# A contrast kernel's first tiles stored in pieces, later tiles loaded two to a DMA, one more sum shared

## The chip, the cores and the metric

The kernel runs on one core of a Trainium2 chip. The metric is the device time of one execution in microseconds (us); three runs of the kernel before gave 238.86, 238.88 and 239.06 us, median 238.88. Profiles are of one execution each and have their own time beside them. Engines are called by the profile's short names: PE is TensorE, DVE is VectorE, ACT is ScalarE, POOL is GpSimd, SP is SyncE. A DMA is issued by an engine's queue (here SP's and ACT's) and carried out by sixteen DMA engines that the queues share.

## What is computed

```python
# x: 16 x 3 x 512 x 512, float32; factor = 1.5
mean = np.mean(x, axis=(2, 3), keepdims=True)
return np.clip(mean + factor * (x - mean), 0, 1).astype(np.float32)
```

For each of 48 images of 262,144 pixels: the mean, then factor * x + (1 - factor) * mean, cut to the range 0 to 1. The input and the output have 50.33 MB each; every byte is read once and written once.

## The kernel before

The input is seen as 12 tiles of 128 partitions by 8192 numbers (`ROW`), 4 MB each. An image fills 32 partitions, so a tile holds four images. SBUF holds a ring of six tiles (`BUFS`); tile t lives in slot t % 6, is changed in place, and is stored from there. A load of tile t + 6 therefore has to wait until tile t has been stored.

A tile goes through these steps:

- `load` (L67 to L75): a DMA issued by SP, for one tile or, with n=2, for two tiles in neighbouring slots. In one for two tiles a partition's row of the first tile is followed by its row of the second, so that both land together.
- `add` (L87 to L91): one ACT pass, a copy onto itself, whose accumulator gives each partition's sum. For tile 0 the work is shared: DVE sums the first 4352 numbers of each partition (`SUM`, the reduction at L109), ACT the other 3840.
- `shift_by` (L93 to L97): PE multiplies the sums by a 128 x 128 matrix `blockw`, which has (1 - factor) / 262144 in four blocks of 32 x 32, so that each partition of the result `bias` in PSUM holds its image's (1 - factor) * mean. A shared sum takes two matmuls into one accumulator.
- `clip` (L77 to L85): two DVE passes, first factor * x + bias (L79), then the cut to 0 and 1 (L83).
- `store` (L99 to L100): a DMA issued by ACT's queue. ACT works its instructions in order, so a store that waits for DVE holds up the ACT pass behind it, and an ACT pass that waits for a load holds up the store behind it.

The order is written by hand (`tc.manual_schedule()`). At the start SP issues the loads of tile 0, of tile 1, of tiles 2 and 3 in one DMA, and of tiles 4 and 5 in one DMA. Tile 0 is then clipped and stored in three pieces of 4, 12 and 16 KB per partition (`CUTS`: columns 0 to 1024, to 4096, to 8192), with the ACT pass for the sum of tile 1 ahead of the last store; then SP issues the load of tile 6. The loop at L120 takes tiles 1 to 11: matmul, clip, the sum of the next tile on ACT, the store of this tile behind it, and the load of tile t + 6 alone. Waits between engines, for landings and for slots are put in by the framework, which also reuses eight semaphores for DMA completions.

Of the kernel before, what the change touches and what calls it, by code (L numbers as in the profile page):

```python
# [1 line left out]

# [4 lines left out]


P = 128  # L10
ROW = 8192
BUFS = 6
SHORT = 2048
CUTS = (0, SHORT // 2, 2 * SHORT, ROW)
SUM = 4352


@with_exitstack
def kernel(
    ctx: ExitStack,  # L20
    tc: tile.TileContext,
    x: bass.AP,
    factor: float,
    out: bass.AP,
):

    nc = tc.nc
    f32 = mybir.dt.float32  # L30
    Alu = mybir.AluOpType
    Act = mybir.ActivationFunctionType

    B, C, H, W = x.shape
    n_img, n_pix = B * C, H * W
    ppi = n_pix // ROW
    per_tile = P // ppi
    n_tiles = n_img // per_tile
    assert ppi * ROW == n_pix and per_tile * n_tiles == n_img

    factor = float(factor)
    wconst = (1.0 - factor) / float(n_pix)

    x_f = x.rearrange("b c h w -> (b c h w)")
    out_f = out.rearrange("b c h w -> (b c h w)")

    def dram(ap, t, c0=0, c1=ROW):
        return bass.AP(tensor=ap.tensor, offset=t * P * ROW + c0, ap=[[ROW, P], [1, c1 - c0]])

    consts = ctx.enter_context(tc.tile_pool(name="consts", bufs=1))  # L50
    xpool = ctx.enter_context(tc.tile_pool(name="xpool", bufs=1))
    small = ctx.enter_context(tc.tile_pool(name="small", bufs=1))
    psum = ctx.enter_context(tc.tile_pool(name="psum", bufs=1, space=bass.MemoryType.PSUM))


    sums = small.tile([P, 2 * n_tiles], f32, name="sums")
    bias = psum.tile([P, n_tiles], f32, name="bias")

    blockw = consts.tile([P, P], f32, name="blockw")
    nc.gpsimd.memset(blockw, 0.0)  # L60
    for a in range(0, P, ppi):
        nc.gpsimd.memset(blockw[a : a + ppi, a : a + ppi], wconst)  # L62


    ring = xpool.tile([P, BUFS, ROW], f32, name="ring")

    def load(t, c0=0, c1=ROW, n=1):  # L67

        b = t % BUFS
        src = bass.AP(  # L70
            tensor=x_f.tensor,
            offset=t * P * ROW + c0,
            ap=[[ROW, P], [P * ROW, n], [1, c1 - c0]],
        )
        nc.sync.dma_start(out=ring[:, b : b + n, c0:c1], in_=src)  # L75

    def clip(t, c0, c1):  # L77
        part = ring[:, t % BUFS, c0:c1]
        nc.vector.tensor_scalar(  # L79
            out=part, in0=part, scalar1=factor, scalar2=bias[:, t : t + 1],  # L80
            op0=Alu.mult, op1=Alu.add,
        )
        nc.vector.tensor_scalar(  # L83
            out=part, in0=part, scalar1=0.0, scalar2=1.0, op0=Alu.max, op1=Alu.min
        )  # L85

    def add(t, c0=0):  # L87
        part = ring[:, t % BUFS, c0:ROW]
        own = sums[:, 2 * t : 2 * t + 1]
        nc.scalar.activation(out=part, in_=part, func=Act.Copy, accum_out=own)  # L90
        return own  # L91

    def shift_by(t, *parts):  # L93
        for k, part in enumerate(parts):
            nc.tensor.matmul(  # L95
                bias[:, t : t + 1], blockw, part, start=k == 0, stop=k == len(parts) - 1
            )  # L97

    def store(t, c0, c1):  # L99
        nc.scalar.dma_start(out=dram(out_f, t, c0, c1), in_=ring[:, t % BUFS, c0:c1])  # L100

    with tc.manual_schedule():
        load(0)
        load(1)
        load(2, n=2)
        load(4, n=2)

        rest = sums[:, 1:2]
        nc.vector.tensor_reduce(  # L109
            out=rest, in_=ring[:, 0, 0:SUM], axis=mybir.AxisListType.X, op=Alu.add  # L110
        )
        shift_by(0, add(0, SUM), rest)
        for c0, c1 in zip(CUTS[:-2], CUTS[1:-1]):
            clip(0, c0, c1)
            store(0, c0, c1)
        clip(0, CUTS[-2], ROW)
        own = add(1)
        store(0, CUTS[-2], ROW)
        load(BUFS)
        for t in range(1, n_tiles):  # L120
            shift_by(t, own)
            clip(t, 0, ROW)
            if t + 1 < n_tiles:
                own = add(t + 1)
            store(t, 0, ROW)
            if t + BUFS < n_tiles:
                load(t + BUFS)


# [1 line left out]
_INS = ['x', 'factor']  # L131
_OUTS = [((16, 3, 512, 512), 'float32')]

_NUMBERS = {'factor': 1.5}


# [26 lines left out]
```

## Time and profile before

| what | value |
|---|---|
| median of three runs | 238.88 us |
| the profiled execution's time / its span | 238.96 / 237.2 us |
| moved by DMA | 100.66 MB, mean 424 GB/s |
| busy: DVE / ACT / PE | 112.1 / 82.9 / 7.6 us |
| last load issued / landed | 162.46 / 195.23 us |
| last store issued / landed | 212.10 / 236.35 us |

The span runs from the first to the last instruction; the rest of an execution's time lies around it. In the page, part 3 gives each DMA queue's packets, megabytes, and the time that its packets took as a share of sixteen engines' span. An answer by windows gives for each stretch its length, the busy time of PE, PEld, DVE, ACT and POOL with the number of instructions, the granted clock, the mean share of the DMA engines that was busy, and GB/s. A line of the timeline gives start, duration, engine, source line, operation, output and input, and in brackets the idle time before it with what ended it. Line numbers of the form L79 are those of the kernel before.

### The profile page before, as it was taken

The numbers are of one execution on the slowest core, as the hardware profiler recorded it, in microseconds if no ns is written. First come the engines' busy times: TensorE is split into PE (matmuls) and PEld (weight loads), VectorE is DVE, ScalarE is ACT, GpSimd is POOL, SyncE is SP. The second block draws the span as 40 slices with busy tenths as digits, with TensorE's granted clock in tenths as the row PEclk, the third lists the DMA queues.
The fourth block names the chain that finished last, engine by engine and source line by source line (L and its number), as shares of the span: only waits on it lengthen the run. The fifth ranks groups of instructions, "written<-read, shape, count | busy, mean of one in ns | idle before, by whom it ended". The sixth has DMA issues, their size and how long they took to land.

```text
span 237.2 us, 219 instructions
## 1 busy us (share of the span) xinstructions
PE 7.6 (3%) x26; PEld 6.5 (3%) x26; DVE 112.1 (47%) x29; ACT 82.9 (35%) x25; POOL 0.9 (0%) x9
## 2 busy tenths in 40 slices
PE   0010000000000000000000000000000000000000
PEld 0010000000000000000000000000000000000000
DVE  0079668008991039979408605902920940770000
ACT  2050910199200696470190083065038009100000
POOL 1000000000000000000000000000000000000000
DMA  7999998999999999999999999999999999999996
GB/s 265 442 442 443 398 473 381 419 456 409 470 387 420 431 442 442 442 442 442 442 437 392 420 431 442 442 442 442 442 437 431 403 420 431 442 442 442 442 442 265
DMA packets 3713, 100.66 MB, mean 424 GB/s; under 512 B 385, under 2 KB 385, under 8 KB 513
## 3 DMA queue, kind: packets, MB, share of 16 engines
q1 hardware_dynamic: 1696, 50.33, 49.7%
q10 hardware_dynamic: 2016, 50.33, 49.2%
q14 instruction: 1, 0.00, 0.0%
HBM read 50.33 MB, written 50.33 MB: 424 GB/s over the span
## 4 chain that ended last, share of the span: by engine, by line
DMA 53%; another core or an unknown queue 14%; DVE 11%; issue 9%; PE 1%; ACT 1%; SPq 0%; ACTq 0%
DMA ring<-in_x_dram 33%; DMA out_dram<-ring 20%; DVE ring L79 6%; DVE ring L83 6%; PE bias L95 1%; ACT ring L90 1%; SPq L75 0%; ACTq L100 0%; ACTq L90 0%
## 5 line engine op out<-in xcount | busy, mean ns | idle before, releaser
L90 ACT ACTIVATE ring<-ring 128x8192 f32<-128x8192 f32 (+1 forms) x12 | 80.7, 6725 | 118.8 <-DMA ring<-in_x_dram 111.5
L79 DVE TENSOR_SCALAR ring<-ring,bias 128x8192 f32<-128x8192 f32 (+3 forms) x14 | 54.3, 3881 | 86.5 <-PE bias L95 86.5
L83 DVE TENSOR_SCALAR ring<-ring 128x8192 f32<-128x8192 f32 (+3 forms) x14 | 53.4, 3818 | 0.5
L95 PE MATMUL bias<-sums,blockw 128*128 128x1 f32 x26 | 7.6, 361 | 195.5 <-ACT ring L90 194.9
L95 PEld LDWEIGHTS bias<-sums,blockw 128*128 128x128 f32 x26 | 6.5, 311 | 196.5 <-ACT ring L90 179.3
L109 DVE TENSOR_REDUCE sums<-ring 128x1 f32<-128x4352 f32 x1 | 4.7, 4686 | 12.9 <-DMA ring<-in_x_dram 12.9
L90 ACT ACTIVATION_READ_ACCUMULATOR ring<-ring 128x1 f32 x12 | 2.2, 186 | 0.0
L90 ACT ACT_TABLE_LOAD x1 | 1.3, 1283 | 0.7 <-PEq L144 0.7
L62 POOL MEMSET blockw<- 32x32 f32 x4 | 0.5, 116 | 0.2
L60 POOL MEMSET blockw<- 128x128 f32 x1 | 0.2, 204 | 0.3 <-POOLq L144 0.3
L144 POOL MEMSET const-bfloat16-1.0<- 128x1 bf16 x1 | 0.1, 111 | 0.0
L144 POOL MEMSET const-uint8-127<- 128x1 uint8 x1 | 0.1, 111 | 0.0
L144 POOL MEMSET const-float32-1.0<- 128x1 f32 x1 | 0.1, 108 | 0.0
L144 POOL MEMSET const-float32-0.0<- 128x1 f32 x1 | 0.1, 103 | 0.2 <-issue 0.2
## 6 DMA issues: line engine op xcount, KB each, us to landing
out_dram<-ring ACTq DMA_DIRECT2D x11, 4096.0 KB, 44.7
ring<-in_x_dram SPq DMA_DIRECT2D x8, 4096.0 KB, 32.7
ring<-in_x_dram SPq DMA_DIRECT2D x2, 8192.0 KB, 60.8
out_dram<-ring ACTq DMA_DIRECT2D x1, 2048.0 KB, 37.3
out_dram<-ring ACTq DMA_DIRECT2D x1, 1536.0 KB, 26.2
out_dram<-ring ACTq DMA_DIRECT2D x1, 512.0 KB, 16.1
```

The lines of the kernel that those rows point to most:

```text
L60: nc.gpsimd.memset(blockw, 0.0)
L62: nc.gpsimd.memset(blockw[a : a + ppi, a : a + ppi], wconst)
L79: nc.vector.tensor_scalar(out=part, in0=part, scalar1=factor, scalar2=bias[:, t : t + 1], op0=Alu.mult, op1=Alu.add,)
L83: nc.vector.tensor_scalar(out=part, in0=part, scalar1=0.0, scalar2=1.0, op0=Alu.max, op1=Alu.min)
L90: nc.scalar.activation(out=part, in_=part, func=Act.Copy, accum_out=own)
L95: nc.tensor.matmul(bias[:, t : t + 1], blockw, part, start=k == 0, stop=k == len(parts) - 1)
L109: nc.vector.tensor_reduce(out=rest, in_=ring[:, 0, 0:SUM], axis=mybir.AxisListType.X, op=Alu.add)
L144: nc = _bacc.Bacc("TRN2", target_bir_lowering=False, num_devices=1)
```

## The change

- Tile 0 is stored in four pieces of 4, 8, 12 and 8 KB per partition, tile 1 in two of 16 KB, tile 2 in two of 20 and 12 KB. `CUTS` is now a table by tile.
- All loads after the first two are DMAs of two tiles: the loads of tiles 6 and 7, 8 and 9, 10 and 11 are issued together, after the store of tile 1, 3 and 5.
- The sum of tile 10 (the eleventh) is shared between DVE and ACT, as that of tile 0 is.
- The order on ACT's queue differs. The stores of tiles 0 to 2 and of the odd tiles come ahead of the next tile's sum, except the last piece of tile 0, which stays behind the sum of tile 1. The stores of even tiles from 4 on come behind the next tile's sum. The sum of tile 1 now stands behind the third piece of tile 0 and not the second.

```diff
-SHORT = 2048
-CUTS = (0, SHORT // 2, 2 * SHORT, ROW)
+CUTS = {0: (0, 1024, 3072, 6144, ROW), 1: (0, 4096, ROW), 2: (0, 5120, ROW)}
...
-    def shift_by(t, *parts):
+    def share(t):
+        rest = sums[:, 2 * t + 1 : 2 * t + 2]
+        nc.vector.tensor_reduce(
+            out=rest, in_=ring[:, t % BUFS, 0:SUM], axis=mybir.AxisListType.X, op=Alu.add
+        )
+        return [add(t, SUM), rest]
+
+    def shift_by(t, parts):
...
+    def pieces(t):
+        cuts = CUTS.get(t, (0, ROW))
+        return zip(cuts, cuts[1:])
...
-        rest = sums[:, 1:2]
-        nc.vector.tensor_reduce(
-            out=rest, in_=ring[:, 0, 0:SUM], axis=mybir.AxisListType.X, op=Alu.add
-        )
-        shift_by(0, add(0, SUM), rest)
-        for c0, c1 in zip(CUTS[:-2], CUTS[1:-1]):
-            clip(0, c0, c1)
-            store(0, c0, c1)
-        clip(0, CUTS[-2], ROW)
-        own = add(1)
-        store(0, CUTS[-2], ROW)
-        load(BUFS)
-        for t in range(1, n_tiles):
+        own = share(0)
+        for t in range(n_tiles):
             shift_by(t, own)
-            clip(t, 0, ROW)
-            if t + 1 < n_tiles:
-                own = add(t + 1)
-            store(t, 0, ROW)
-            if t + BUFS < n_tiles:
-                load(t + BUFS)
+            for c0, c1 in pieces(t):
+                clip(t, c0, c1)
+                if t % 2 or t in CUTS:
+                    if t == 0 and c1 == ROW:
+                        own = [add(1)]
+                    store(t, c0, c1)
+            if 0 < t < n_tiles - 1:
+                own = share(t + 1) if t + 1 == n_tiles - 2 else [add(t + 1)]
+            if t % 2 == 0 and t not in CUTS:
+                store(t, 0, ROW)
+            if t % 2 and t + BUFS < n_tiles:
+                load(t + BUFS - 1, n=2)
```

## The prediction

> **What bounds the kernel now.** I read the page's queue table first, then the busy rows of two stretches, then the timeline around the first and last stores, then the DMA packet records of the trace (start, length and bytes of each). The page's third part, queue, packets, MB, share of the 16 DMA engines:
>
> ```profile
> q1 hardware_dynamic: 1696, 50.33, 49.7%
> q10 hardware_dynamic: 2016, 50.33, 49.2%
> ```
>
> q1 carries SP's loads, q10 ACT's stores. Together they hold the sixteen engines 98.9% of the span. Two long stretches (length, busy time by engine, granted clock, DMA share, GB/s):
>
> ```profile
> 4.00:196.00 192.00, 7.01 (x24) 6.01 (x24) 103.21 (x27) 75.18 (x23) 0.00 (x0) 1.00 1.00 432
> 196.00:234.00 38.00, 0.59 (x2) 0.50 (x2) 8.92 (x2) 6.44 (x2) 0.00 (x0) 1.00 0.99 429
> ```
>
> The rate is the same with loads and stores mixed and, after 196 us, with stores alone. In the packet records an engine moves one 32 KB row of one partition in 1.213 us, load or store, and the next starts 0.004 us before that ends: 1.209 us a row. With both queues filled, the two take turns row by row, and a DMA's closing 4-byte packet uses up a turn. From 1.75 us (first packet) to 236.00 us (last) no engine has a gap over 0.05 us. Of the rows, 96 loads and 96 stores to an engine, 192 x 1.209 = 232.1 us; the rest of 234.25 us is the staggered, slow first packets and two patches, at 34 to 38 and 64 to 67 us, where load rows ran long by 0.3 us per engine each.
>
> The tail, by the timeline:
>
> ```profile
> 195.31 7.03 ACT L90 ACTIVATE ring<-ring 128x8192 f32<-128x8192 f32 x1 [12.25 <-DMA ring<-in_x_dram]
> 195.36 0.34 ACTq L100 DMA_DIRECT2D out_dram<-ring  x1
> ...
> 207.64 4.43 DVE L83 TENSOR_SCALAR ring<-ring 128x8192 f32<-128x8192 f32 x1
> 212.10 0.34 ACTq L100 DMA_DIRECT2D out_dram<-ring  x1
> ```
>
> The last load lands at 195.23 us, the last store is issued at 212.10 and lands at 236.35; the store ahead of it lands only at 226.68. So the last store waits in its queue, not for its data. The chain of waits ends in those last instructions because it follows semaphores; the queues bind. Nothing here can gain unless it takes bytes or idle time from the DMA engines, and the only slack is the two patches, 0.6 us.
>
> **The change, part by part.** All sums go against the profiled execution, 238.96 us, with a span of 237.2 us; it stands 0.08 us above the median of 238.88.
>
> *Pieces of the first three tiles.* Rows of 4, 12, 16 and 32 KB take 0.159, 0.460, 0.611 and 1.213 us: in proportion to bytes plus 8.4 ns, 4 ns of it overlapped, so 4.4 ns a packet. Stores of tiles 0 to 2 go from 24 + 8 + 8 = 40 packets an engine to 32 + 16 + 16 = 64. That is 24 x 4.4 ns = 0.11 us, on the path. Closing packets stay the same in number (17 stores for 14, 7 loads for 10). VectorE gets six more passes over pieces (two each for one more piece of tiles 0, 1 and 2); a pass has about 0.2 us fixed (0.759 us for 1024, 4.491 for 8192), so 1.2 us in all, beside an engine that is idle more than half the span: nothing, as long as stores stay queued.
>
> *Order on ACT's queue.* Now the third piece of tile 0 goes out ahead of the sum of tile 1, which then starts at about 26.4 instead of 23.71 us; queued behind it are the fourth piece and, through the matmul, tile 1's clip. Tile 1's two stores are issued ahead of the sum of tile 2 (now its store sits behind that sum until 46.47, though its clip ended at 40.46). Estimate from the rows: issues of tile 0 at 19.8, 22.3, 26.0, 33.7, tile 1 at 39 and 43.7, tile 2 at 59.3 and 63.0. Tile 0's 32 turns alone last until about 72 us, so the store queue is never empty; cost 0. Were that cover gone, each microsecond without stores would only go to loads as long as those last (about 71 us).
>
> *Loads in pairs.* Turns are shared by rows, and small store rows give loads a larger share: tiles 4 and 5 land at about 71 instead of 78.87 us. The built order shows one new wait: the load of tiles 4 and 5 waits for tile 1's landing (a reused semaphore), so it is issued at 22.6 instead of 2.10. Behind it on SP stand only loads that wait longer; the 16 rows of tiles 2 and 3 fill q1 until 45: nothing. Then the load of 6 and 7 waits for both tile 0 and tile 1 to be stored (about 81 us); q1 is empty from 71 to 85, and q10 alone runs, with tiles 1 and 2 queued and tile 3 from 80 on. A single queue moves 429 GB/s, so an empty q1 costs nothing. The same for 8 and 9 (issued when tile 3 has landed, 120 us; tiles 4 and 5 issued at 97 and 106) and 10 and 11 (after tile 5, 155 us, with 8 and 9 still in the queue).
>
> *The tail, the one place where it is near.* After the last load lands, tiles 10 and 11 both have to be summed and clipped, while only what is queued covers them. Tile 9's store must end after the same work as before (96 load rows, 80 store rows): 217.01 less 0.36 from last packet to landing, plus 0.11, is 216.75. The last load: tile 3's store ends 80 rows earlier, 216.75 - 80 x 1.209 = 120.0, lands at 120.4, and the load of 8 and 9 is issued. How long until its rows run? The nearest row is the first store: issued at 19.79 into a busy engine, its first packets ran at 23.2 (two engines) and 24.2 to 24.6 (fourteen), so 3.4 to 4.8 us. From 123.8 to 125.2, 32 load rows alternate with some 30 store rows: 62 x 1.209 = 75.0, and 0.4 to the landing: 199.2 to 200.6. Then, as for tile 0, reduction, matmul and waits (12.89 to 18.27: 5.4), two passes (4.49 + 4.43 and gaps: 8.95), issue: 14.4 us, tile 10's store is issued at 213.6 to 215.0. Into an empty queue the first load needed 1.0 us on the first engine and 2.0 on the last (0.74 to 1.75 and 2.71). So its rows are ready between 214.6 and 217.0, against 216.75: room of 2.1 down to minus 0.3 us. I take the middle, 1 us of room, since fourteen of sixteen engines showed the long wait and most of them the short start. The shared sum is what makes the room: by ScalarE alone 7.03 + 0.19 and 0.86 for the matmul, some 2.6 us later. Tile 11: 8.95 us after tile 10, 223 to 224, while tile 10's store runs to 226.4: covered.
>
> Sum: 238.96 + 0.11 = 239.07, **239.1 us**, 0.1% above the median.
>
> **One rule against the row.** The three more stores could each cost a fixed time. In the trace, the first store's last packet is followed at once by a load row, the second store's packets by turns; no gap stands at any change of DMA. Uncovered, a change of DMA would cost 1.0 us from issue to first packet and 0.36 to the landing: 3 x 1.36 = 4.1 us, 243.1; the three loads saved give nothing back, since theirs is covered now. The Trainium skill, "DMA: Bandwidth & Descriptors", section "Anatomy of one DMA — SWDGE (gpsimd) path", gives about 2.0 us fixed to each DMA, and its "Rules for kernel authors" want 1 MiB or more in each, where the first pieces have 0.5 and 1; by that figure the estimate would be 6 us, 245. The trace so far disagrees, as the other queue covers it.
>
> **The rivals.**
>
> *A. The engines stay filled: 239.1.* For it: q10 has a backlog at every point of the sum, and each landing of before follows from turns of 1.209 us.
>
> *B. The tail runs dry: slower.* If the last load lands under 15.4 to 16.4 us (14.4 and 1.0 to 2.0) ahead of the end of tile 9's store, the engines idle between tiles 9 and 10. It decides at a landing later than 200.4 to 201.4. One more row of delay, 1.21 us on the middle, takes the room and about 0.2 more; two, 1.4 us. So 239.3 to 240.5, typically 239.8. Against: the slowest wait seen is already in the bounds.
>
> *C. The long load rows multiply: slower.* Both patches fell in loads of two tiles (2 of 2; none over 0.02 us in the single loads after the start), and both just when a store with small rows had ended and all sixteen engines read at once (2 of 3 such ends). If it is the pairs, five instead of two cost 3 x 0.3 = 0.9 us: 240.0. If it is the ends of small stores, one or two more: 239.4 to 239.7.
>
> *D. The patches vanish: 239.07 - 0.6 = 238.5*, the floor; that is 0.17% under the median, and more is not there to be had.
>
> *E. Each piece pays its own start: 243.1*, above.
>
> **The numbers.** A measurement of this kernel tells 0.2% (0.48 us: 238.40 and 239.36) from no change. Chances: A 0.50, B 0.22, C 0.20, D 0.05, E 0.03. B, C and E come out slower almost throughout (0.44 of 0.45, taken as 0.45); half of D, where the patches give a little more than they cost before, is faster by more than the bound, 0.03, and the rest joins A as no change, 0.52. Range 238.5 to 240.6: D below, the dear end of B and C above; outside are E, two causes at once, and more than two late rows.
>
> **What would show it.** Right: packets without a gap from 1.75 us to the end; tiles 4 and 5 land near 71, 6 and 7 near 115, 8 and 9 near 163, 10 and 11 near 200 us; tile 10's store is issued near 214 and tile 9's lands near 217; the rate is 432 GB/s in every stretch. B: a stretch near 216 us with a DMA share well under 1, and the last two stores later by as much. C: stretches under 410 GB/s more than twice, each inside a load of two tiles, or at the ends of pieces. E: gaps at each change of DMA before 80 us. I am wrong in the ground if rows of a pair or of small pieces take longer than their bytes say, or if a queue alone runs slower than 429 GB/s.

## The result: 0.63% slower, inside the range and beside the likeliest case

The changed kernel takes 240.42 us (median of six runs, 240.2 to 241.17) against 238.87 us in six runs of the kernel before: ratio 1.0063, 95% interval 1.0051 to 1.0074. The forecast was 239.1 us, no change; that is 1.3 us too low. The range of 238.5 to 240.6 holds the result. The profiled execution took 240.38 us with a span of 238.4, so the span grew by 1.2 of the 1.4 us. In this document a run's ratio is always to runs of the kernel before on the same chip, over undisturbed executions; only the kernel before with all loads of one tile had others, three of six at 252.1 to 253.2 us, its profiled one among them.

The changed kernel's page, part 3, the two queues:

```profile
q1 hardware_dynamic: 1648, 50.33, 49.6%
q10 hardware_dynamic: 2448, 50.33, 49.1%
```

and the same two stretches by windows:

```profile
4.00:196.00 192.00, 6.42 (x22) 5.51 (x22) 95.07 (x31) 67.27 (x20) 0.00 (x0) 1.00 1.00 430
196.00:234.00 38.00, 1.76 (x6) 1.51 (x6) 22.43 (x5) 10.51 (x4) 0.00 (x0) 1.00 1.01 436
```

Both queues together are still busy 98.7% of the span, and the DMA share is 1.00 in both stretches. So neither stretch was lost to idle engines. The tail by the timeline:

```profile
200.47 4.69 DVE L94 TENSOR_REDUCE sums<-ring 128x1 f32<-128x4352 f32 x1 [11.84 <-DMA ring<-in_x_dram]
...
214.94 9.15 ACTq L106 DMA_DIRECT2D out_dram<-ring  x2
219.28 4.43 DVE L82 TENSOR_SCALAR ring<-ring 128x8192 f32<-128x8192 f32 x1
```

The last load has landed at 200.45 us, tile 10's store is issued at 214.94 and tile 11's 9 us later (223.74); tile 9's store lands at 218.24. That is the forecast's timetable (200, 214, 217) to within 1.3 us, and nothing runs dry. But tile 9's store lands 1.2 us later than before (217.01), so most of the time was lost ahead of the tail.

The difference shows at the very end. Two windows of the kernel before, from 234 us on:

```profile
234.00:235.00 1.00, 0.00 (x0) 0.00 (x0) 0.00 (x0) 0.00 (x0) 0.00 (x0) 1.00 1.21 524
235.00:238.00 3.00, 0.00 (x0) 0.00 (x0) 0.00 (x0) 0.00 (x0) 0.00 (x0) 1.00 0.00 0
```

and of the changed kernel:

```profile
234.00:235.00 1.00, 0.00 (x0) 0.00 (x0) 0.00 (x0) 0.00 (x0) 0.00 (x0) 1.00 0.99 426
235.00:238.00 3.00, 0.00 (x0) 0.00 (x0) 0.00 (x0) 0.00 (x0) 0.00 (x0) 1.00 0.15 66
```

A row is counted where it starts, so a share over 1 is rows that end a little later. Before, practically all sixteen DMA engines start their last row before 235 us. After the change, the share of 0.15 over 3 us is 66 x 3 = 198 KB, six rows: some engines are still at work while the others are done. The packet records give it exactly: the closing packets of the last store (4 bytes, one from each engine) come at 235.60 to 235.99 us before (mean 235.76), and at 235.81 to 237.26 after (mean 236.22). The mean engine is 0.46 us later, the slowest 1.27.

### The profile page after: what moved, and what is told of

Its sections match the earlier page's. It is cut to its first block, busy times and chain, and to the rows that moved or that the text cites. A ratio compares the mean times of both kernels' runs of the same rounds, so it can differ in the third digit from the quotient of the medians.

```text
span 238.4 us, 232 instructions
## 1 busy us (share of the span) xinstructions
PE 8.2 (3%) x28; PEld 7.0 (3%) x28; DVE 117.5 (49%) x36; ACT 79.1 (33%) x25; POOL 0.9 (0%) x9
## 3 DMA queue, kind: packets, MB, share of 16 engines
q1 hardware_dynamic: 1648, 50.33, 49.6%
## 4 chain that ended last, share of the span: by engine, by line
DMA 35%; DVE 17%; another core or an unknown queue 15%; issue 3%; PE 1%; SPq 0%; ACTq 0%; ACT 0%; DVEq 0%
DMA ring<-in_x_dram 18%; DMA out_dram<-ring 17%; DVE ring L78 8%; DVE ring L82 8%; DVE sums L94 2%; PE bias L101 1%; SPq L74 0%; ACTq L106 0%; ACT ring L89 0%; DVEq L78 0%
## 5 line engine op out<-in xcount | busy, mean ns | idle before, releaser
L89 ACT ACTIVATE ring<-ring 128x8192 f32<-128x8192 f32 (+1 forms) x12 | 77.0, 6420 | 131.2 <-DMA ring<-in_x_dram 100.9
L78 DVE TENSOR_SCALAR ring<-ring,bias 128x8192 f32<-128x8192 f32 (+5 forms) x17 | 55.0, 3233 | 80.9 <-PE bias L101 80.9
L82 DVE TENSOR_SCALAR ring<-ring 128x8192 f32<-128x8192 f32 (+5 forms) x17 | 53.9, 3172 | 0.6
L94 DVE TENSOR_REDUCE sums<-ring 128x1 f32<-128x4352 f32 x2 | 9.4, 4686 | 24.7 <-DMA ring<-in_x_dram 24.7
L101 PE MATMUL bias<-sums,blockw 128*128 128x1 f32 x28 | 8.2, 362 | 203.4 <-ACT ring L89 202.3
L101 PEld LDWEIGHTS bias<-sums,blockw 128*128 128x128 f32 x28 | 7.0, 312 | 204.5 <-ACT ring L89 186.7
```

What stands on the lines that cost most here:

```text
L78: nc.vector.tensor_scalar(out=part, in0=part, scalar1=factor, scalar2=bias[:, t : t + 1], op0=Alu.mult, op1=Alu.add,)
L82: nc.vector.tensor_scalar(out=part, in0=part, scalar1=0.0, scalar2=1.0, op0=Alu.max, op1=Alu.min)
L94: nc.vector.tensor_reduce(out=rest, in_=ring[:, t % BUFS, 0:SUM], axis=mybir.AxisListType.X, op=Alu.add)
L101: nc.tensor.matmul(bias[:, t : t + 1], blockw, part, start=k == 0, stop=k == len(parts) - 1)
```

## The experiments

Three theories stood at first. *Tail*: tiles 10 and 11 are stored too late. *Pairs*: loads of two tiles have long rows. *Pieces*: stores with short rows beside loads make rows long and pull the engines apart. "Long rows" below is the time that rows took over what their bytes cost, after the first 5 us, summed and divided by sixteen engines: 0.69 us before, 1.07 after, nearly all of it in the first 110 us. "Spread" is the largest time from the first to the last of the sixteen engines in the landing of any one DMA: 1.6 us before, 2.9 after.

### First four

**Late loads one tile to a DMA.**

```diff
-            if t % 2 and t + BUFS < n_tiles:
-                load(t + BUFS - 1, n=2)
+            if t + BUFS < n_tiles:
+                load(t + BUFS)
```

> The new pieces, order and shared sum, with tiles 6 to 11 loaded one tile to a DMA. Theory 'pieces' (long load rows and engines out of step come while stores with rows under 32 KB run): the loss stays, 240.0 to 240.6 us, long rows up to about 105 us, closing packets of the last store over 1 us apart. Theory 'pairs' (they come from loads of two tiles): back to 239.1 to 239.4, no long rows after 70 us. Theory 'tail' (the stores of tiles 10 and 11 come late): tile 11 lands near 195 us, so the loss goes too, 239.1.

Measured: 242.88 us, ratio 1.0155 (1.0133 to 1.0177). All three expectations were too low, and the loss more than doubled. Long rows 2.51 us, spread 4.7 us. Tile 11 landed at 195.4 us and its store was issued in good time, so *tail* falls here; and without the late pairs the new pieces cost more, not less.

**The kernel before with all loads of one tile.**

```diff
-        load(2, n=2)
-        load(4, n=2)
+        for t in range(2, BUFS):
+            load(t)
```

> The kernel before with all loads of one tile, the first six too. 'Pairs': the patches at 35 and 65 us vanish, 0.6 us less, 238.3. 'Pieces': the patches stay where the first and third store end, 238.9. 'Tail': 238.9.

Measured: ratio 1.0138 (1.0111 to 1.0166), 242.1 to 243.0 us in three runs, of which there is no profile. No theory expected this: taking the two pairs away, with no short row added, costs more than the whole change. For these loads *pairs* is refuted, with the sign turned around.

**The changed kernel with the old stores of tiles 0 to 2.**

```diff
-CUTS = {0: (0, 1024, 3072, 6144, ROW), 1: (0, 4096, ROW), 2: (0, 5120, ROW)}
+CUTS = {0: (0, 1024, 4096, ROW), 1: (0, ROW), 2: (0, ROW)}
```

> The changed kernel with the stores of before for tiles 0 to 2 (pieces of 4, 12 and 16 KB, then whole tiles); pairs, new order and shared sum stay. 'Pieces': long rows only up to about 70 us, 238.9 to 239.3. 'Pairs': five loads of two tiles, 240.0 to 240.5. 'Tail': the last load still lands near 200 us and tile 10 is issued near 215, so 240.4.

Measured: 239.59 us (238.99 to 240.4, 12 runs), ratio 1.0022 (1.0009 to 1.0036). Most of the loss is gone, as *pieces* has it, but the median is over the 239.3 us that *pieces* allowed, and the runs lie far apart. The profiled execution (239.0 us, one of the two shortest of the twelve) has long rows of 0.56 us, all before 70 us, and a span of 237.2 us, that of the kernel before. From 84 to 108 us it does the same things at the same time as the changed kernel:

```profile
84.00:108.00 24.00, 1.17 (x4) 1.00 (x4) 17.74 (x4) 10.97 (x4) 0.00 (x0) 1.00 1.01 437
```

and the changed kernel:

```profile
84.00:108.00 24.00, 1.17 (x4) 1.00 (x4) 17.75 (x4) 10.44 (x4) 0.00 (x0) 1.00 1.02 427
```

Equal work on DVE, a full DMA share in both, and 437 against 427 GB/s: the engines are as busy, but get less done.

**Tile 10 summed by ACT alone.**

```diff
-                own = share(t + 1) if t + 1 == n_tiles - 2 else [add(t + 1)]
+                own = [add(t + 1)]
```

> The changed kernel with tile 10 summed by ScalarE alone, which puts the store of tile 10 some 2.6 us later (217.5 instead of 214.94). 'Tail': what is lost now grows by all of it, 243.0. 'Pieces' and 'pairs': tile 9's packets end at 216.5 to 217.9 in the changed kernel, its rows would now start at 218.5 to 219.5, an idle stretch of 1 to 2.5 us: 241.5 to 242.5, of which the earliest engines wait most.

Measured: 240.73 us, ratio 1.0070 (1.0046 to 1.0095); its profiled execution has a span of 239.6 us. Both expectations were too high. The idle time did come; the same kernel in two stretches, and below them the changed kernel in the first:

```profile
210.00:222.00 12.00, 0.58 (x2) 0.50 (x2) 11.97 (x3) 5.34 (x2) 0.00 (x0) 1.00 0.84 363
222.00:234.00 12.00, 0.00 (x0) 0.00 (x0) 4.78 (x2) 0.00 (x0) 0.00 (x0) 1.00 1.02 437
```

```profile
210.00:222.00 12.00, 0.59 (x2) 0.50 (x2) 11.93 (x4) 0.98 (x2) 0.00 (x0) 1.00 1.01 434
```

A share of 0.84 over 12 us is 1.9 us lost by the mean engine, as tile 10's store came at 217.99. But all engines had to wait for it, and the last store's closing packets then lie within 0.16 us (238.30 to 238.46) instead of 1.45. The wait took up part of what the engines were apart: against the changed kernel's profiled execution the slowest engine closes 1.2 us later, not 1.9. What the shared sum is worth isn't settled: this profiled execution (241.51 us) is the second longest of six, and over all runs the interval of the ratio overlaps that of the changed kernel.

### Second four

**Order and shared sum alone** (old stores, late loads of one tile: the edits of the first and the third run together).

> The changed kernel's order and shared sum, with the stores of before for tiles 0 to 2 and with tiles 6 to 11 loaded one tile to a DMA: what is left of the change is order and shared sum alone. Theory 'pieces' (stores with rows under 32 KB stretch load rows and pull the engines apart): 238.9 to 239.2, the last store's closing packets within 0.5 us. Theory 'singles' (late loads of one tile stretch rows, pairs less so; the new pieces only add): 239.8 to 242, closing packets over 1 us apart.

Measured: 239.19 us, ratio 1.0009 (1.0000 to 1.0018), spread 1.8 us, long rows 0.41, the last closing packets 0.63 us apart (within 0.5 was expected). No loss: *singles* as such cost nothing here, so what they cost in the first run hangs on the new pieces beside them.

**Only tile 0's new pieces.**

```diff
-CUTS = {0: (0, 1024, 3072, 6144, ROW), 1: (0, 4096, ROW), 2: (0, 5120, ROW)}
+CUTS = {0: (0, 1024, 3072, 6144, ROW), 1: (0, ROW), 2: (0, ROW)}
```

> The changed kernel with only tile 0 in the new four pieces, tiles 1 and 2 whole. 'Pieces', if the loss grows with the number of small rows: 8 of the 24 added packets, 239.7 to 240.0. If it is the rows of tile 2 (20 and 12 KB) beside the loads of tiles 6 and 7 that matter: 239.4 to 239.6, as with the old pieces.

Measured: 240.37 us, ratio 1.0057 (1.0045 to 1.0069), spread 2.8 us: more than either reading gave, and as much as the whole change.

**Only tiles 1 and 2 in the new pieces.**

```diff
-CUTS = {0: (0, 1024, 3072, 6144, ROW), 1: (0, 4096, ROW), 2: (0, 5120, ROW)}
+CUTS = {0: (0, 1024, 4096, ROW), 1: (0, 4096, ROW), 2: (0, 5120, ROW)}
```

> The changed kernel with tile 0 in the old three pieces, tiles 1 and 2 in the new ones. 'Pieces', by number: 16 of the 24 added packets, 239.9 to 240.2. If it is tile 2's rows: all of the loss, 240.3 to 240.6, with long rows near 85 to 105 us.

Measured: 240.88 us, ratio 1.0071 (1.0054 to 1.0088), spread 4.6 us. That is above the higher expectation, and with only 0.12 us of long rows between 85 and 110 us. Either half costs as much as both (1.0063), so the loss isn't a price by the row: that reading of *pieces* is refuted. And long rows come to 0.63 us here, less than before the change; fifteen engines close the last store within 0.15 us (235.84 to 235.99), one at 237.66. In the windows that one engine is left alone, with a row of 33 KB in each microsecond:

```profile
235.00:236.00 1.00, 0.00 (x0) 0.00 (x0) 0.00 (x0) 0.00 (x0) 0.00 (x0) 1.00 0.08 33
236.00:237.00 1.00, 0.00 (x0) 0.00 (x0) 0.00 (x0) 0.00 (x0) 0.00 (x0) 1.00 0.08 33
```

What counts here is not how much longer rows run in all, but that it falls on one engine. (Eleven of the others had idled 0.06 to 0.37 us at 216.4 us, waiting for tile 10's store, which also drew them together.)

**Other HBM addresses** (and, as it turned out, other packets).

```diff
-                              offset=t * P * ROW + c0, ap=[[ROW, P], [1, c1 - c0]]
+                              offset=t * ROW + c0, ap=[[12 * ROW, P], [1, c1 - c0]]
...
-            ap=[[ROW, P], [P * ROW, n], [1, c1 - c0]],
+            ap=[[12 * ROW, P], [ROW, n], [1, c1 - c0]],
```

> The changed kernel with other HBM addresses alone: a tile takes every twelfth row of 32 KB of input and output, not 128 neighbouring ones, so a partition's rows of all tiles lie side by side, 384 KB from the next partition's. It sums other groups of rows than images. Theory 'addresses' (long rows come from which HBM rows are read and written at the same time): their number and places change much, and the time moves by over 0.5 us either way (238.8 to 239.5 if they vanish, 241 to 245 if they multiply). If they come from the queues or from SBUF: the same rows at the same places, 240.2 to 240.7.

Measured: 240.75 us, ratio 1.0078 (1.0065 to 1.0091). The places of the long rows changed: none at 35 us, 0.63 us at 60 to 65, 0.36 at 125, 0.22 at 160. The time did not follow: it stayed with the changed kernel's, though a move by over 0.5 us was expected. Spread 3.3 us. But the edit did more than its description says. The page's part 3 has 640 packets fewer for the loads (1648 in the changed kernel):

```profile
q1 hardware_dynamic: 1008, 50.33, 49.6%
```

In a load of two tiles a partition's two rows now lie side by side in HBM as well as in SBUF, and the packet records have them as one packet of 64 KB (2.418 us). So loads and stores also take turns in another way: tiles 2 and 3 land at 43.2 us, not 45.6, and the first piece of tile 0 at 43.4, not 35.8. Whether the long rows moved by the addresses or by the packets, this run can't tell.

### Third four

By now the packet records suggested another theory, *step*: in the kernels without a loss the sixteen engines keep step (mostly thirteen or more of them move load rows at a time, and then store rows), and in those with a loss they are at different turns. The records can be put into sixteen chains, as within an engine a row starts 3 or 4 ns before the one ahead of it ends; each chain has 96 load rows and the bytes of 96 rows in stores, so no engine takes work off another. A landing needs all sixteen closing packets; so each transfer ends with the slowest engine, and so does the kernel.

**The changed kernel again.**

> The changed kernel once more, unchanged, for a second profile. Theory 'step' (the engines lose step: where loads and stores begin at different turns on different engines, each transfer waits for its slowest engine): 240.2 to 240.8, the landings of tiles 6 to 11 again over 2 us from first to last engine, the last store's closing packets again over 0.8 us apart, though not in the same amounts. Theory 'fixed places' (the long rows hang on the place in the program alone): the same amounts of long rows at 35, 85 to 90 and 100 us, to 0.05.

Measured: 240.83 us, ratio 1.0085 (1.0066 to 1.0104), at the upper edge of what *step* gave. Its other sign failed: the loads of tiles 6 to 11 land 1.2 to 2.0 us from first to last engine (0.95 to 0.98 in the first profile), not over 2. The long rows stand at the same places, but not in the same amounts: 0.44 us at 85 (0.16 in the first profile), 0.46 at 100 (0.40). Spread 4.1 us, the last closing packets 1.47 us apart.

**The kernel before at the other addresses** (the edit of the run above).

> The kernel before with other HBM addresses alone: rows of a tile 384 KB apart, as in the changed kernel with rows apart; it sums other groups of rows than images. 'Step': its load queue never runs empty before the last load, the engines keep step, 238.8 to 239.3. 'Addresses': long rows move or multiply, 239.8 to 241, about as the changed kernel with rows apart (240.75).

Measured: 238.81 us, ratio 0.9998 (0.9989 to 1.0006). It has long rows too, 0.60 us at 60 to 65, but all engines keep step throughout, with a spread of 0.4 us. Here too the two loads of two tiles run in packets of 64 KB (256 packets fewer). In neither kernel did the new layout move the time, which speaks against *addresses* as its cause, as far as an edit can that changes two things; *step* fits.

**The kernel before with tile 0 stored whole.**

```diff
-CUTS = (0, SHORT // 2, 2 * SHORT, ROW)
+CUTS = (0, ROW)
```

> The kernel before with tile 0 stored whole: all rows are of 32 KB. 16 packets fewer (0.07 us), and no small store ends beside loads. 'Step': the load queue stays filled, 238.3 to 238.9, closing packets within 0.5 us; the lower end if the patches at 35 and 65 us, which stood at the ends of the first and third piece, go too. The start of the stores at 30 instead of 20 us costs nothing as long as loads are queued. 'Pieces cover the start' (stores that begin late leave the engines idle at the end): 239.5 or more.

Measured: 239.77 us, ratio 1.0041 (1.0025 to 1.0056), over what *step* allowed. The time is one that the other theory gave, but not for its reason: tile 11's store is issued at 219.77 us, tile 10's lands at 227.1, and no engine idles. The load queue never runs empty, and yet the engines lose step from about 60 us on (mostly six against ten at a time), with a spread of 1.9 us, and the last closing packets are 0.86 us apart. So an empty load queue isn't needed to lose step, and this version isn't better either.

**The changed kernel with all tiles stored whole.**

```diff
-CUTS = {0: (0, 1024, 3072, 6144, ROW), 1: (0, 4096, ROW), 2: (0, 5120, ROW)}
+CUTS = {0: (0, ROW), 1: (0, ROW), 2: (0, ROW)}
```

> The changed kernel with all tiles stored whole; pairs, order and shared sum stay. 'Step': no small rows, but the load queue still runs empty before tiles 6 and 7, or 8 and 9, and begins again among stores: 239.3 to 240.4, with landings over 1.5 us from first to last engine. 'Small rows' (only they cost): 238.5 to 239.1.

Measured: 241.56 us, ratio 1.0116 (1.0092 to 1.0141), with no short row at all. *Small rows* is refuted, since long rows come to 1.3 us without any, and *step* was too low as well. But most of this loss is idle time: here rival B of the prediction comes true. The last load lands at 203.31 us, 3 us after that of the changed kernel, tile 10's store is issued at 217.79, and the queue has run dry, for 1.8 us on the mean engine:

```profile
210.00:222.00 12.00, 0.59 (x2) 0.50 (x2) 11.97 (x3) 3.90 (x2) 0.00 (x0) 1.00 0.83 358
```

The runs side by side, by the ratio to the kernel before:

| run | ratio | profiled execution, us | spread, us | long rows, us | of the engine that closes last, us | last closings apart, us |
|---|---|---|---|---|---|---|
| before, other addresses | 0.9998 | 238.80 | 0.4 | 0.67 | 0.8 | 0.40 |
| before | 1 | 238.96 | 1.6 | 0.69 | 0.9 | 0.40 |
| order and shared sum alone | 1.0009 | 239.15 | 1.8 | 0.41 | 0.3 | 0.63 |
| changed, old stores | 1.0022 | 239.00 | 1.6 | 0.56 | 0.6 | 0.34 |
| before, tile 0 whole | 1.0041 | 239.51 | 1.9 | 0.90 | 1.1 | 0.86 |
| only tile 0's pieces | 1.0057 | 240.30 | 2.8 | 1.41 | 1.6 | 1.04 |
| changed | 1.0063 | 240.38 | 2.9 | 1.07 | 1.8 | 1.45 |
| only pieces of tiles 1, 2 | 1.0071 | 240.76 | 4.6 | 0.63 | 2.2 | 1.82 |
| changed, other addresses | 1.0078 | 240.64 | 3.3 | 1.62 | 2.3 | 1.28 |
| changed, again | 1.0085 | 240.60 | 4.1 | 1.37 | 1.6 | 1.47 |
| changed, single late loads | 1.0155 | 242.30 | 4.7 | 2.51 | 3.5 | 2.18 |

(All columns but the ratio are of the one profiled execution; the ratio is of all runs. Left out are the two runs whose tail ran dry and the one without a profile. The sixth column is of one of the sixteen chains; where two chains fit a record equally well they can be mixed up, so it is good to a few tenths.)

The time goes with the long rows of the engine that closes last: at most 1.1 us of them in the executions up to 239.5 us, 1.6 or more in those from 240.3 us on. It doesn't go with the long rows in all: 0.63 us of them cost 0.7% in one kernel, and 0.67 us cost nothing in another. Nor does *step* order the kernels. From 78 to 195 us thirteen or more engines move the same kind of row in 86% of the time before, in 78% in the changed kernel and in 88% with only the pieces of tiles 1 and 2, which lose; and in 32% in the kernel before with tile 0 whole, which loses less.

## Why the range held and the sum was wrong, step by step

**What bounds the kernel: right.** Two queues share sixteen busy engines, and there was nothing to gain. No kernel of the study that computes the reference came out faster than before.

**Pieces, 0.11 us: right as far as it went.** Rows of 8 and 20 KB took 0.309 and 0.761 us, by the law of bytes plus 8.4 ns. On the mean engine the rest of the 0.46 us is long rows: 1.07 against 0.69, 0.38 more. By the prediction's own sign this is where it was wrong in the ground: in the changed kernel 20 KB store rows at 85 us took up to 0.38 us over what their bytes say, and load rows of a pair up to 0.94.

**Order, pairs, tail: right.** Landings were forecast near 71, 115, 163 and 200 us and came at 71.0, 117.4, 162.9 and 200.5, at most 2.4 us late. The new wait of the load of tiles 4 and 5 moved its issue to 22.58 us and cost nothing; the queue that ran alone from 72 us held the engines at 100.8% between 72 and 84. Rival B did not happen in the changed kernel, with no gap between tiles 9 and 10, though it was near: a landing 3 us later let it happen in the last run.

**Each piece pays its own start (rival E): no.** The rows of the three more stores follow without a gap of over 0.1 us, and the change cost 1.55 us where this rival put 4.1. The Trainium skill, "DMA: Bandwidth & Descriptors", section "Anatomy of one DMA — SWDGE (gpsimd) path", gives about 2.0 us fixed to a DMA on that path, an estimate of 6 us for three; the trace of this case, whose DMAs are issued by SP and ACT with others queued beside them, shows no such cost.

**The step that failed is the sum itself**, "238.96 + 0.11", and under it the sentence "Tile 9's store must end after the same work as before (96 load rows, 80 store rows)". It reckoned with one engine that stands for sixteen. With 1.75 to 236.00 us and no gap, every engine had been equally late, so I took the mean for the slowest. After the change the mean engine ends 0.46 us later, where 0.11 was forecast, and the slowest engine lies 1.04 us over the mean (237.26 over 236.22) where it lay 0.23 (235.99 over 235.76): 0.81 us more. 0.46 + 0.81 = 1.27 us, against a span that grew by 1.2. What stood in the place of "the same work" is rows that ran long: the engine that closes last has 1.8 us of them, 0.94 in a single load row at 104.3 us, where it had 0.9 before. In the second profile of the changed kernel the two parts are 0.85 and 0.60 us, so both errors count: long rows put at no more than before, and the mean taken for the slowest.

That the range held was luck in part. Its upper end, 240.6, came from rival B, which did not happen; rival C, the nearer one, ended at 240.0, under the measured 240.42. The likeliest case, no change, did not come.

Rival C was the nearest. It saw long rows multiply and gave 239.4 to 240.0, but named the wrong owners: pairs (refuted in the first four runs) or the ends of small stores (the largest patch of the changed kernel, 0.40 us at 103 us, does follow the end of a 12 KB store, yet kernels with short and with whole rows both have such patches). Its sign, stretches under 410 GB/s more than twice, could not have told: of the page's forty slices, first and last left out, six are under 410 before and four after. Above all it priced the long rows on the mean, and missed that they fall more on some engines than on others. That engines can be apart at a share of 1.00 could be seen in the trace of before: in the landings of its loads, fourteen engines kept step and two were a turn behind.

**What stays open.** That the new pieces bring most of the loss is shown by putting the old ones in their place (though tile 0 stored whole, without any piece, loses too); that it is the long rows of the slowest engine is read from the packet records and was not tested by itself. How the engines come apart in the changed kernel can be seen: the spread is 0.6 us at the landing of 81 us, 1.8 at that of 91 and 2.9 at that of 107, and between them the load of tiles 6 and 7 comes into an empty queue, with rows 0.05 to 0.38 us long at 85 to 86.5 us, on some of the engines only. The kernel with the old stores goes through the same restart with all engines within 0.3 us and no long row there. But a kernel whose load queue never ran empty lost step too. And why rows run long at some places, on some engines more than on others, and whether HBM addresses have a part in it, no run tells; nor why loading tiles 2 to 5 singly costs 1.4% in the kernel before.

## What to carry to other kernels

Where queues bind, look at the engines one by one, not at their mean share: a share of 1.00 hides engines that are apart, and the last microseconds of the DMA row (a share that falls off in steps instead of at once) show it. A change that adds no bytes and opens no gap can still lose when rows run long on one engine more than on the others, and its cost doesn't add up by parts: each half of the pieces cost as much as both. So such orders are tried on the chip, with enough runs, and a mean sum of rows is a floor for them, not a forecast.

## What the hardware showed that I had not expected

- Sixteen engines with the same bytes ended 0.40 us apart in one order of the same transfers, and 2.18 us in another (late loads one tile to a DMA).
- Rows of 32 KB, 1.213 us as a rule, took up to 2.15 us in the changed kernel; where they ran long changed with a layout that gave other HBM addresses and packets of 64 KB (35 us in one layout, 60 to 65, 125 and 160 us in the other).
- Idle time can cost less than it lasts: 1.9 us of it before tile 10's store brought the engines together to 0.16 us, and the slowest engine closed 1.2 us later.
- Two rows that are neighbours in HBM and in SBUF ran as one packet of 64 KB, 2.418 us, with nothing in the kernel asking for it.
